# Weaving the first two chunks of three weight stages: w_out, w_up and the w_down quarters of a hybrid decoder layer

## The chip, the cores and the metric

One core of a Trainium2 chip runs the whole layer in one launch. The metric is the device time of that launch in microseconds (us); less is better. The kernel before takes 1529.46 us, the median of 3 runs (1527.65 to 1530.21).

## The reference, cut to what matters

One decoder layer over 256 tokens of width 2048, all in float32. Three branches (S5, RG-LRU, stick-breaking attention) are merged under gates; what matters here comes behind them:

```
merged = g_s5*(y_s5 @ w_br_s5) + g_lru*(y_lru @ w_br_lru) + g_attn*(y_attn @ w_br_attn)
h  = x + merged @ w_out                       # 2048 x 2048
hn = rms_norm(h, norm_mlp_g)
h  = h + (relu(hn @ w_up) ** 2) @ w_down      # 2048 x 8192, 8192 x 2048
out = rms_norm(h, final_norm_g)
```

## The kernel before, in words

**Units.** All weights come as one stream of units of 256 rows by 512 columns (512 KB). SP loads a unit into a raw tile (3 buffers, `load_next`, L110 to L120). `split_next` (L122) turns it into two float32r tiles: ScalarE (ACT) casts raw to hi (L135), VectorE (DVE) subtracts hi from raw and gets lo (L136); this subtraction is called the split below. TensorE then multiplies three times per operand pair: activation hi by weight hi (L213), hi by lo (L214), lo by hi (L215). One unit is 12 matmuls with 512 columns each. hi and lo have 3 buffers, so the cast of unit u waits until TensorE has done unit u-3, and runs in the time of unit u-2.

**Chunks.** `chunk_tok` (L204) computes 512 output columns for both blocks of 128 tokens into two PSUM banks. A chunk of w_out has 8 units (2048 rows). w_up has 16 chunks of 8 units, taken in four quarters; after each quarter of w_up, w_down takes the same quarter of the hidden channels: 4 chunks of 8 units, added to h_tok. `psm` has four banks of this kind.

**What stands between chunks.** The next stage contracts over the columns that a chunk just made, so they have to be transposed and split again before they can be an operand. That is side work, written as generators that are given to `later(gens, rate)` and advanced by `pump()` after each unit, `rate` steps per unit:

- `split_tok(c)` (L848): transposes a chunk of merged (16 DVE transposes of 32x256, four to a step), then splits it into mg_yhi and mg_ylo, the operand of w_out.
- `residual(c)` (L886): after a chunk of w_out is added to the residual (two h_tok additions on DVE, L899): 16 transposes into hT, then hhi (ACT, L883) and hlo (DVE, L884), the operand of w_up.
- `hidden` (L967): after the relu of a chunk of w_up (ACT, L986): 16 transposes into reluT, hd_hi (ACT square, L970), the same square on GpSimd (L971), and hd_lo (DVE, L974), the operand of w_down.
- `norm2` (L907): once the last residual is done, squares and sums hT, one small matmul for the sums over partitions (L914), an rsqrt. Its result is first used by the evacuation of w_down (L929).

The four chunks that feed a stage are read as kt 0 to 15, four kt to a chunk, two kt to a unit. So the last chunk's side work is due in unit 6 of the next stage's first chunk. `ms`, `hs` and `hs_` enforce that: at kt 12 they call `finish`, which issues what is left of the task. That is why the last task of each kind had rate 2:

```
    last = later([split_tok(3, ...)], 2.0)                          # L870
        rq = later([residual(c)], 2.0 if c == 3 else 1.0)           # L900
            hq = later([hidden(...)], 2.0 if c == FQ // CH - 1 else 1.0)   # L988
```

Each engine runs its instructions in order. What order the side work gets among the casts and splits is set where it is pumped, by `issue_after` on the unit's last cast, split and matmul.

Of the kernel before, what the change touches and what calls it, by code (L numbers as in the profile page):

```python
# [46 lines left out]
def hybrid_block(ctx: ExitStack, tc: tile.TileContext, io, out):  # L47
# [156 lines left out]
    def chunk_tok(name, c, k, xs, hold=0, done=None):  # L204
# [702 lines left out]
    def norm2():  # L907
        while rq[0]:
# [67 lines left out]
    for q in range(NQ):  # L976
        hd = {}
        for c in range(FQ // CH):
            banks = chunk_tok("w_up", q * (FQ // CH) + c, D, hs)
# [18 lines left out]
        for c in range(4):  # L998
            if q == NQ - 1 and c == 3:
                chunk_tok("w_down", c, FQ, hs_, HOLD, finish_tokens)  # L1000
                break
            banks = chunk_tok("w_down", c, FQ, hs_)
# [76 lines left out]
```

## Time and profile before

| | |
|---|---|
| median of 3 runs (lowest to highest) | 1529.46 us (1527.65 to 1530.21) |
| the profiled execution: its own time, its span | 1528.9 us, 1527.0 us |
| TensorE (PE) busy | 1491.6 us, 98% |
| VectorE (DVE) busy | 1170.1 us, 77% |
| ScalarE (ACT) busy | 780.2 us, 51% |
| GpSimd (POOL) busy | 113.2 us, 7% |
| DMA | 292.41 MB, mean 191 GB/s |
| granted TensorE clock, mean | 0.993 |

The span is the time from the first to the last instruction; the execution's own time is 1.9 us more. Busy times are sums over the whole span, and say nothing yet about who waits for whom: for that the waits and the timelines of single stages are read. A line "DVE L136 lo<-raw,hi" is the split of a unit.

### The profile page before, as it was taken

Reading aid. Unit: us, or ns where it says so; the run is one execution under the profiler, and the core shown is the slowest. Engines: PE = TensorE matmul, PEld = TensorE weight load, DVE = VectorE, ACT = ScalarE, POOL = GpSimd, SP = SyncE. Lnnn points to the kernel's source line nnn. Section 1 sums busy time; section 2 is a strip of 40 time slices with the busy share of each in tenths; the row PEclk is TensorE's granted clock in tenths of the full one; section 3 lists DMA queues with packets and bytes.
Section 4 is the critical chain, followed back from the end, with each engine's and each line's share of the span. In section 5 each row is a group of like instructions: output and inputs, shape, how many; then the busy total and the mean of one; then the engine's idle time right before and its main releaser. Section 6 shows DMA issues by size and latency. Waiting matters only on the chain.

```text
span 1527.0 us, 19937 instructions
## 1 busy us (share of the span) xinstructions
PE 1491.6 (98%) x7518; PEld 1261.0 (83%) x7518; DVE 1170.1 (77%) x1428; ACT 780.2 (51%) x918; POOL 113.2 (7%) x100
## 2 busy tenths in 40 slices
PE   9898999999998999999999999999999999999997
PEld 9896888989887877987788878888788887888786
DVE  5886998897988989688889885568754886558855
ACT  7478556565765564544346443344433443344443
POOL 6300000000000100001000000000100000000111
PEclk9999999999999999999999999999999999999999
DMA  9454766665565756665765656656566666666564
GB/s 290 143 173 143 227 209 193 194 184 167 172 184 168 209 184 204 187 203 182 250 200 184 184 181 210 191 187 193 193 193 193 192 194 186 195 187 198 176 203 152
DMA packets 88914, 292.41 MB, mean 191 GB/s; under 512 B 12786, under 2 KB 17010, under 8 KB 88562
## 3 DMA queue, kind: packets, MB, share of 16 engines
q1 hardware_dynamic: 88386, 287.93, 60.9%
q10 hardware_dynamic: 432, 3.21, 0.6%
q8 instruction: 59, 0.97, 0.3%
q14 instruction: 37, 0.30, 0.1%
HBM read 282.71 MB, written 2.10 MB: 187 GB/s over the span
## 4 chain that ended last, share of the span: by engine, by line
PE 83%; DVE 9%; ACT 3%; issue 3%; DMA 2%; SPq 0%; DVEq 0%; ACTq 0%
PE mt_w_up L215 7%; PE mt_w_up L214 7%; PE mt_w_up L213 7%; PE mt_w_down L214 7%; PE mt_w_down L215 7%; PE mt_w_down L213 7%; PE mt_w_in L214 5%; PE mt_w_in L215 5%; PE mt_w_in L213 5%; PE mm_w_in L198 4%; PE mm_w_in L199 4%; PE mm_w_in L197 4%; DVE lo L136 4%; ACT hi L135 2%; DVE reluT L683 1%
## 5 line engine op out<-in xcount | busy, mean ns | idle before, releaser
L136 DVE TENSOR_TENSOR lo<-raw,hi 128x1024 fp32r<-128x1024 f32 (+1 forms) x521 | 657.2, 1265 | 305.9 <-ACT hi L135 297.1
L135 ACT CAST hi<-raw 128x1024 fp32r<-128x1024 f32 (+1 forms) x521 | 545.5, 1049 | 643.3 <-PE mt_w_down L215 165.3
L214 PE MATMUL mt_w_down<-lo,hd_hi 128*128 128x512 f32 (+1 forms) x528 | 202.5, 384 | 5.6 <-DVE lo L136 5.6
L213 PE MATMUL mt_w_down<-hi,hd_hi 128*128 128x512 f32 (+1 forms) x528 | 202.1, 383 | 0.0
L215 PE MATMUL mt_w_down<-hi,hd_lo 128*128 128x512 f32 (+1 forms) x528 | 202.0, 383 | 0.0
L214 PE MATMUL mt_w_up<-lo,hhi 128*128 128x512 f32 x512 | 199.3, 389 | 0.0
L215 PE MATMUL mt_w_up<-hi,hlo 128*128 128x512 f32 x512 | 199.2, 389 | 0.0
L213 PE MATMUL mt_w_up<-hi,hhi 128*128 128x512 f32 x512 | 199.2, 389 | 0.0
L214 PE MATMUL mt_w_in<-lo,xhi 128*128 128x512 f32 x448 | 176.3, 394 | 4.2 <-DVE lo L136 4.1
L213 PE MATMUL mt_w_in<-hi,xhi 128*128 128x512 f32 x448 | 177.3, 397 | 2.9 <-ACT hi L135 2.9
L215 PE MATMUL mt_w_in<-hi,xlo 128*128 128x512 f32 x448 | 175.3, 391 | 0.0
L199 PE MATMUL mm_w_in<-xhi,lo 128*128 128x256 f32 x512 | 145.8, 286 | 3.1 <-DVE lo L136 3.0
L197 PE MATMUL mm_w_in<-xhi,hi 128*128 128x256 f32 x512 | 146.3, 286 | 1.7 <-DVE rs L298 0.9
L198 PE MATMUL mm_w_in<-xlo,hi 128*128 128x256 f32 x512 | 145.8, 285 | 0.0
L214 PEld LDWEIGHTS mt_w_down<-lo,hd_hi 128*128 128x128 f32 x528 | 99.2, 188 | 26.6 <-DVE lo L136 7.3
L213 PEld LDWEIGHTS mt_w_down<-hi,hd_hi 128*128 128x128 f32 x528 | 99.2, 188 | 19.5
L215 PEld LDWEIGHTS mt_w_down<-hi,hd_lo 128*128 128x128 f32 x528 | 99.2, 188 | 19.3
L683 DVE STREAM_TRANSPOSE reluT<-relu 32x256 f32<-32x256 f32 x256 | 111.5, 436 | 4.1
L214 PEld LDWEIGHTS mt_w_up<-lo,hhi 128*128 128x128 f32 x512 | 96.1, 188 | 20.1
L213 PEld LDWEIGHTS mt_w_up<-hi,hhi 128*128 128x128 f32 x512 | 96.1, 188 | 19.9
L215 PEld LDWEIGHTS mt_w_up<-hi,hlo 128*128 128x128 f32 x512 | 96.1, 188 | 19.9
L214 PEld LDWEIGHTS mt_w_in<-lo,xhi 128*128 128x128 f32 x448 | 84.6, 189 | 25.0 <-DVE lo L136 8.6
(278 smaller groups left out, 2039.5 us busy)
## 6 DMA issues: line engine op xcount, KB each, us to landing
raw<-in_w_in SPq DMA_DIRECT2D x175, 512.0 KB, 4.1
raw<-in_w_up SPq DMA_DIRECT2D x128, 512.0 KB, 4.0
raw<-in_w_down SPq DMA_DIRECT2D x128, 512.0 KB, 4.3
raw<-in_w_out SPq DMA_DIRECT2D x32, 512.0 KB, 4.3
raw<-in_w_br_lru SPq DMA_DIRECT2D x16, 512.0 KB, 4.2
raw<-in_w_br_attn SPq DMA_DIRECT2D x16, 512.0 KB, 4.1
raw<-in_w_br_s SPq DMA_DIRECT2D x16, 512.0 KB, 4.1
stk<-ux SPq DMA_DIRECT2D x96, 64.0 KB, 3.9
```

Of the source, the lines that this page charges most:

```text
L135: anchor["act"] = nc.scalar.copy(h[:, k, :], r[:, k, :]).ins
L136: anchor["dve"] = nc.vector.tensor_tensor(l_[:, k, :], r[:, k, :], h[:, k, :].bitcast(F32), ALU.subtract).ins
L197: nc.tensor.matmul(o, wh[:, kk, s], xh, start=first and ct % 2 == 0, stop=False, skip_group_check=True)
L198: nc.tensor.matmul(o, wh[:, kk, s], xl, start=False, stop=False, skip_group_check=True)
L199: mm = nc.tensor.matmul(o, wl[:, kk, s], xh, start=False, stop=last and ct % 2 == 1, skip_group_check=True)
L213: nc.tensor.matmul(banks[j], xh[:, s], wh[:, a:b], start=kt == 0, stop=False)
L214: nc.tensor.matmul(banks[j], xh[:, s], wl[:, a:b], start=False, stop=False)
L215: return nc.tensor.matmul(banks[j], xl[:, s], wh[:, a:b], start=False, stop=kt == ng * UK - 1)
L683: nc.vector.transpose(d_[32 * a:32 * a + 32, :, :, 32 * b:32 * b + 32], s_[32 * b:32 * b + 32, :, :, 32 * a:32 * a + 32])
```

## The change

In w_out, in the first quarter of w_up, and in each quarter of w_down, chunks 0 and 1 become a pair (`pair_tok`) that holds all four PSUM banks: units 0 to 5 of chunk 0, units 0 to 5 of chunk 1, then units 6 and 7 of chunk 0 and units 6 and 7 of chunk 1. The stream of loads is reordered in the same way (`add_pair`). kt 12 is now first read in unit 12 of sixteen. Chunk 0 is done after unit 14, chunk 1 after unit 16 (before: 8 and 16), and what follows a chunk (`out_done`, `up_done`, `down_done`) is the old code as a function. The three tasks that had rate 2 have rate 1. Quarters 1 to 3 of w_up keep their chunks one by one.

```diff
+    LATE = 2
+    def add_pair(name, c, k, g0=0):
+        ng = k // (P * UK)
+        for gs_ in (range(ng - LATE), range(ng - LATE, ng)):
+            stream.extend((name, c + i, g0 + g) for i in range(2) for g in gs_)
+    add_pair("w_out", 0, D)
+    for c in range(2, 4):
         add("w_out", c, D)
...
+        if q == 0:
+            add_pair("w_up", 0, D)
+        for c in range(0 if q else 2, FQ // CH):
             add("w_up", q * (FQ // CH) + c, D)
+        add_pair("w_down", 0, FQ, q * (FQ // (P * UK)))
...
+    def pair_tok(name, c, k, xs, done):
+        ng = k // (P * UK)
+        banks = [[psm.tile([P, CH], F32, tag="mm", ...) for t in range(2)] for i in range(2)]
+        for gs_ in (range(ng - LATE), range(ng - LATE, ng)):
+            for i in range(2):
+                for g in gs_:
+                    (nm, cc, _), wh, wl = next_unit()
...
+                    anchor["pe"] = mm.ins
+                    pump()
+                if gs_.stop == ng:
+                    done(c + i, banks[i])
...
-    last = later([split_tok(3, mlp.tile(...))], 2.0)
+    last = later([split_tok(3, mlp.tile(...))], 1.0)
...
-        rq = later([residual(c)], 2.0 if c == 3 else 1.0)
+        rq[0] = later([residual(c)], 1.0)
+    pair_tok("w_out", 0, D, ms, out_done)
+    for c in range(2, 4):
+        out_done(c, chunk_tok("w_out", c, D, ms))
...
-            hq = later([hidden(r, h_[:, k, :], l_[:, k, :], f"{q}_{c}")], 2.0 if c == FQ // CH - 1 else 1.0)
+            hq[0] = later([hidden(r, h_[:, k, :], l_[:, k, :], f"{q}_{c}")], 1.0)
+        if q == 0:
+            pair_tok("w_up", 0, D, hs, up_done)
...
+        pair_tok("w_down", 0, FQ, hs_, down_done)
```

The instructions are the same in kind and number, but for the grouping of transposes. Three places in DVE's order are shown, since DVE makes lo for TensorE and does the transposes. The number behind lo is the unit's place in the stream: w_out begins with 232, the first quarter of w_up with 264, the first quarter of w_down with 296. x8 is two steps of a task, or of two tasks, without anything between. Line numbers of the changed kernel are its own (L147 is the old L136, L716 the old L683, L917 the old L884, L933 the old L899, L1012 the old L974).

First place, DVE behind chunk 0 of w_out, the residual of chunk 0. Before:

```order
L136 TENSOR_TENSOR lo243_6816<-raw243_6795,hi243_6815 128x1024
L683 STREAM_TRANSPOSE hT_6622<-h_tok_6625 32x2x4x32 x4
L136 TENSOR_TENSOR lo244_6838<-raw244_6813,hi244_6837 128x1024
L683 STREAM_TRANSPOSE hT_6622<-h_tok_6625 32x2x4x32 x4
L136 TENSOR_TENSOR lo245_6860<-raw245_6835,hi245_6859 128x1024
L683 STREAM_TRANSPOSE hT_6622<-h_tok_6625 32x2x4x32 x4
L136 TENSOR_TENSOR lo246_6882<-raw246_6857,hi246_6881 128x1024
L683 STREAM_TRANSPOSE hT_6622<-h_tok_6625 32x2x4x32 x4
```

Now, units 17 to 22 of w_out, the residuals of chunks 0 and 1:

```order
L147 TENSOR_TENSOR lo249_6924<-raw249_6903,hi249_6923 128x1024
L716 STREAM_TRANSPOSE hT_6622<-h_tok_6625 32x2x4x32 x4
L933 TENSOR_TENSOR h_tok_6625<-mp_w_out_1_0_232_6629,xres_6619 128x512
L933 TENSOR_TENSOR h_tok_6625<-mp_w_out_1_1_232_6630,xres_6619 128x512
L147 TENSOR_TENSOR lo250_6950<-raw250_6921,hi250_6949 128x1024
L716 STREAM_TRANSPOSE hT_6622<-h_tok_6625 32x2x4x32 x4
L147 TENSOR_TENSOR lo251_6972<-raw251_6947,hi251_6971 128x1024
L716 STREAM_TRANSPOSE hT_6622<-h_tok_6625 32x2x4x32 x8
L147 TENSOR_TENSOR lo252_6998<-raw252_6969,hi252_6997 128x1024
L716 STREAM_TRANSPOSE hT_6622<-h_tok_6625 32x2x4x32 x8
L147 TENSOR_TENSOR lo253_7024<-raw253_6995,hi253_7023 128x1024
L917 SCALAR_TENSOR_TENSOR hlo_6624<-hT_6622,par_79,hhi_6623 128x256 x2
```

The two tasks have met: twice eight transposes stand between two splits, and after split 253 (unit 21) and split 254 an hlo pair of the first task and four transposes of the second stand together.

Second place, DVE in the first quarter of w_up, hidden tasks (relu0_0 is chunk 0, relu0_1 chunk 1). Before, chunk 1 alone:

```order
L136 TENSOR_TENSOR lo282_7682<-raw282_7656,hi282_7681 128x1024
L683 STREAM_TRANSPOSE reluT0_1_7697<-relu0_1_7674 32x2x4x32 x4
L136 TENSOR_TENSOR lo283_7705<-raw283_7679,hi283_7704 128x1024
L683 STREAM_TRANSPOSE reluT0_1_7697<-relu0_1_7674 32x2x4x32 x4
L136 TENSOR_TENSOR lo284_7727<-raw284_7702,hi284_7726 128x1024
```

Now, units 18 to 22 of w_up:

```order
L147 TENSOR_TENSOR lo282_7671<-raw282_7641,hi282_7670 128x1024
L716 STREAM_TRANSPOSE reluT0_0_7636<-relu0_0_7615 32x2x4x32 x4
L716 STREAM_TRANSPOSE reluT0_1_7690<-relu0_1_7663 32x2x4x32 x4
L147 TENSOR_TENSOR lo283_7698<-raw283_7668,hi283_7697 128x1024
L716 STREAM_TRANSPOSE reluT0_0_7636<-relu0_0_7615 32x2x4x32 x4
L716 STREAM_TRANSPOSE reluT0_1_7690<-relu0_1_7663 32x2x4x32 x4
L147 TENSOR_TENSOR lo284_7724<-raw284_7695,hi284_7723 128x1024
L716 STREAM_TRANSPOSE reluT0_1_7690<-relu0_1_7663 32x2x4x32 x4
L147 TENSOR_TENSOR lo285_7748<-raw285_7721,hi285_7747 128x1024
L716 STREAM_TRANSPOSE reluT0_1_7690<-relu0_1_7663 32x2x4x32 x4
L147 TENSOR_TENSOR lo286_7770<-raw286_7745,hi286_7769 128x1024
L1012 TENSOR_TENSOR hd_lo0_0_7614<-reluT0_0_7636,hd_hi0_0_7613 128x1024
```

Here too two tasks stand side by side: two groups of eight, where there were groups of four.

Third place, DVE at the start of the first quarter of w_down, the hidden task of the last w_up chunk. Before:

```order
L136 TENSOR_TENSOR lo298_8022<-raw298_7996,hi298_8021 128x1024
L683 STREAM_TRANSPOSE reluT0_3_8037<-relu0_3_8014 32x2x4x32 x8
L136 TENSOR_TENSOR lo299_8049<-raw299_8019,hi299_8048 128x1024
L683 STREAM_TRANSPOSE reluT0_3_8037<-relu0_3_8014 32x2x4x32 x8
L136 TENSOR_TENSOR lo300_8075<-raw300_8046,hi300_8074 128x1024
```

Now:

```order
L147 TENSOR_TENSOR lo298_8024<-raw298_7996,hi298_8023 128x1024
L716 STREAM_TRANSPOSE reluT0_3_8039<-relu0_3_8014 32x2x4x32 x4
L147 TENSOR_TENSOR lo299_8047<-raw299_8021,hi299_8046 128x1024
L716 STREAM_TRANSPOSE reluT0_3_8039<-relu0_3_8014 32x2x4x32 x4
L147 TENSOR_TENSOR lo300_8069<-raw300_8044,hi300_8068 128x1024
L716 STREAM_TRANSPOSE reluT0_3_8039<-relu0_3_8014 32x2x4x32 x4
L147 TENSOR_TENSOR lo301_8091<-raw301_8066,hi301_8090 128x1024
L716 STREAM_TRANSPOSE reluT0_3_8039<-relu0_3_8014 32x2x4x32 x4
L147 TENSOR_TENSOR lo302_8113<-raw302_8088,hi302_8112 128x1024
```

The sixteen transposes are spread over four units instead of two. It is the same in the other quarters.

## Rows read from the trace of the kernel before

In timelines the columns are: start in us from the span's start, duration in us (of a group of x instructions, of all of them), engine, line, operation, out<-in, shapes, count, and in brackets the idle time of the engine just before and what ended it.

**Rows 1.** The page's first part: span, and TensorE's busy time, share and instructions.
```profile
span 1527.0 us, 19937 instructions
PE 1491.6 (98%) x7518; PEld 1261.0 (83%) x7518; DVE 1170.1 (77%) x1428; ACT 780.2 (51%) x918; POOL 113.2 (7%) x100
```

**Rows 2.** The list of waits of TensorE from 722 us (start of w_out) to the end: who waited for whom, us in total, times, longest.
```profile
PE mt_w_down L214 <- DVE lo L136: 5.6, 4, 1.4
PE mt_w_out L214 <- DVE lo L136: 2.4, 3, 1.5
PE ps_n L914 <- DVE hT L313: 0.9, 1, 0.9
```

**Rows 3.** Timeline of TensorE: first matmul of w_down, the first matmul of its unit 4 and the two behind it; last, the same place in the fourth quarter.
```profile
901.77 0.39 PE L213 MATMUL mt_w_down<-hi,hd_hi 128*128 128x512 f32 x1
...
912.65 0.39 PE L213 MATMUL mt_w_down<-hi,hd_hi 128*128 128x512 f32 x1
914.44 0.50 PE L214 MATMUL mt_w_down<-lo,hd_hi 128*128 128x512 f32 x1 [1.40 <-DVE lo L136]
914.77 0.39 PE L215 MATMUL mt_w_down<-hi,hd_lo 128*128 128x512 f32 x1
...
1441.80 0.50 PE L214 MATMUL mt_w_down<-lo,hd_hi 128*128 128x512 f32 x1 [1.41 <-DVE lo L136]
```

**Rows 4.** Timeline of DVE at the same place, splits of units 2, 3, 4 and 5 of w_down and one of the two groups of transposes between them.
```profile
903.54 1.22 DVE L136 TENSOR_TENSOR lo<-raw,hi 128x1024 fp32r<-128x1024 f32 x1 [1.98 <-ACT hi L135]
...
908.28 1.22 DVE L136 TENSOR_TENSOR lo<-raw,hi 128x1024 fp32r<-128x1024 f32 x1
909.54 3.59 DVE L683 STREAM_TRANSPOSE reluT<-relu 32x256 f32<-32x256 f32 x8
913.16 2.36 DVE L136 TENSOR_TENSOR lo<-raw,hi 128x1024 fp32r<-128x1024 f32 x2
```

**Rows 5.** Timeline of DVE at the end of w_out: splits with an hlo pair between them, the additions behind the last chunk, and the split of unit 2 of w_up.
```profile
807.51 1.23 DVE L136 TENSOR_TENSOR lo<-raw,hi 128x1024 fp32r<-128x1024 f32 x1
808.65 0.87 DVE L884 SCALAR_TENSOR_TENSOR hlo<-hT,par,hhi 128x256 fp32r<-128x256 f32 x2
809.44 1.22 DVE L136 TENSOR_TENSOR lo<-raw,hi 128x1024 fp32r<-128x1024 f32 x1
...
812.85 1.28 DVE L899 TENSOR_TENSOR h_tok<-mt_w_out,xres 128x512 f32<-128x512 f32 x2
814.38 1.23 DVE L136 TENSOR_TENSOR lo<-raw,hi 128x1024 fp32r<-128x1024 f32 x1 [0.25 <-ACT hi L135]
```

**Rows 6.** Timeline of TensorE: first matmul of w_up, and the norm's small matmul with the one ahead of it.
```profile
813.09 0.39 PE L213 MATMUL mt_w_up<-hi,hhi 128*128 128x512 f32 x1
...
838.93 0.39 PE L213 MATMUL mt_w_up<-hi,hhi 128*128 128x512 f32 x1
840.24 0.58 PE L914 MATMUL ps_n<-ones,hT 128*128 128x1 f32 x4 [0.92 <-DVE hT L313]
```

**Rows 7.** Timeline of ACT in w_up: a cast with nothing in its way, the relu of chunk 0 and the cast behind it, the table load and the rsqrt of the norm, a hidden square.
```profile
816.01 1.05 ACT L135 CAST hi<-raw 128x1024 fp32r<-128x1024 f32 x1 [1.67 <-PE mt_w_up L215]
...
834.37 1.28 ACT L986 ACTIVATE relu<-mt_w_up 128x512 f32<-128x512 f32 x2 [0.28 <-PE mt_w_up L215]
835.55 1.06 ACT L135 CAST hi<-raw 128x1024 fp32r<-128x1024 f32 x1
...
839.37 1.28 ACT L296 ACT_TABLE_LOAD   x1
840.85 0.26 ACT L296 ACTIVATE rs<-ps_n,eps_t 128x2 f32<-128x2 f32 x1 [0.20 <-PE ps_n L914]
...
893.95 1.06 ACT L970 ACTIVATE hd_hi<-reluT 128x1024 fp32r<-128x1024 f32 x1 [1.81 <-DVE reluT L683]
```

**Rows 8.** Timeline of DVE in a w_up chunk with a hidden task at rate 1: two splits with four transposes between them, and a split a little later.
```profile
884.73 1.22 DVE L136 TENSOR_TENSOR lo<-raw,hi 128x1024 fp32r<-128x1024 f32 x1
885.98 1.78 DVE L683 STREAM_TRANSPOSE reluT<-relu 32x256 f32<-32x256 f32 x4
887.79 1.23 DVE L136 TENSOR_TENSOR lo<-raw,hi 128x1024 fp32r<-128x1024 f32 x1
...
895.99 2.15 DVE L136 TENSOR_TENSOR lo<-raw,hi 128x1024 fp32r<-128x1024 f32 x1 [0.81 <-ACT hi L135]
```

**Rows 9.** Timeline of GpSimd, two of its squares of reluT.
```profile
895.16 1.90 POOL L971 TENSOR_TENSOR reluT<-reluT 128x1024 f32<-128x1024 f32 x1 [19.62 <-ACT hd_hi L970]
914.36 2.91 POOL L971 TENSOR_TENSOR reluT<-reluT 128x1024 f32<-128x1024 f32 x1 [17.31 <-ACT hd_hi L970]
```

**Rows 10.** Timeline of TensorE in w_out: its first matmul, and the matmuls on lo of unit 5 and of unit 8.
```profile
722.72 0.39 PE L213 MATMUL mt_w_out<-hi,mg_yhi 128*128 128x512 f32 x1
...
738.84 0.50 PE L214 MATMUL mt_w_out<-lo,mg_yhi 128*128 128x512 f32 x1 [0.28 <-DVE lo L136]
...
747.86 0.50 PE L214 MATMUL mt_w_out<-lo,mg_yhi 128*128 128x512 f32 x1 [0.54 <-DVE lo L136]
```

**Rows 11.** Timeline of ACT in w_out: the casts of units 5 and 8.
```profile
736.48 1.05 ACT L135 CAST hi<-raw 128x1024 fp32r<-128x1024 f32 x1 [7.06 <-DMA raw<-in_w_out]
...
745.50 1.05 ACT L135 CAST hi<-raw 128x1024 fp32r<-128x1024 f32 x1 [4.81 <-DMA raw<-in_w_out]
```

**Rows 12.** DMA queues from 727 to 737 us: packets, MB, share of 16 engines. q10 is the queue on which ACT issues (here the residual input xres).
```profile
q10 hardware_dynamic: 144, 2.10, 58.2%
```

More of the change, by code (lines that the diff above doesn't have):

```diff
@@ L85, in hybrid_block @@
         add(*(("w_br_s5", int(a[1]), W) if a[0] == "b" else ("w_in", GATE0 + int(a[1]), D)))
-    for c in range(4):
+    LATE = 2
[5 more added lines that the diff above has]
+    for c in range(2, 4):
         add("w_out", c, D)
@@ L232, in chunk_tok @@
         return banks
+    def pair_tok(name, c, k, xs, done):
+        ng = k // (P * UK)
+        banks = [[psm.tile([P, CH], F32, tag="mm", name=f"mp_{name}_{c + i}_{t}_{st['use']}") for t in range(2)] for i in range(2)]
+        for gs_ in (range(ng - LATE), range(ng - LATE, ng)):
+            for i in range(2):
+                for g in gs_:
+                    (nm, cc, _), wh, wl = next_unit()
+                    assert (nm, cc) == (name, c + i)
+                    for kk in range(UK):
+                        kt = g * UK + kk
+                        xh, xl = xs(kt)
+                        for t in range(2):
+                            s = slice(t * P, (t + 1) * P)
+                            o = banks[i][t]
+                            nc.tensor.matmul(o, xh[:, s], wh[:, kk, :], start=kt == 0, stop=False)
+                            nc.tensor.matmul(o, xh[:, s], wl[:, kk, :], start=False, stop=False)
+                            mm = nc.tensor.matmul(o, xl[:, s], wh[:, kk, :], start=False, stop=kt == ng * UK - 1)
+                    anchor["pe"] = mm.ins
+                    pump()
+                if gs_.stop == ng:
+                    done(c + i, banks[i])
     par = const.tile([P, sum(PAR.values())], F32, name="par")
@@ L869, in hybrid_block @@
     nc.scalar.dma_start(x_tok, io["x_res"])
-    last = later([split_tok(3, mlp.tile([P, 4, L], F32, tag="reluT", name="mT3", bufs=2))], 2.0)
+    last = later([split_tok(3, mlp.tile([P, 4, L], F32, tag="reluT", name="mT3", bufs=2))], 1.0)
     hT = act.tile([P, KT, L], F32, tag="m16", name="hT")
@@ L894, in hybrid_block, with out_done @@
     rs2 = const.tile([P, 2], F32, name="rs2")
-    for c in range(4):
-        banks = chunk_tok("w_out", c, D, ms)
+    rq = [None]
+    def out_done(c, banks):
         s = slice(c * CH, (c + 1) * CH)
@@ L899, in hybrid_block @@
             nc.vector.tensor_tensor(h_tok[:, t, s], banks[t], x_tok[:, t, s], ALU.add)
-        rq = later([residual(c)], 2.0 if c == 3 else 1.0)
+        rq[0] = later([residual(c)], 1.0)
+    pair_tok("w_out", 0, D, ms, out_done)
+    for c in range(2, 4):
+        out_done(c, chunk_tok("w_out", c, D, ms))
     def hs(kt):
         if kt >= 12:
-            finish(rq)
+            finish(rq[0])
         return hhi[:, kt, :], hlo[:, kt, :]
     def norm2():
-        while rq[0]:
+        while rq[0][0]:
             yield
@@ L976, in hybrid_block, with up_done @@
     for q in range(NQ):
-        hd = {}
-        for c in range(FQ // CH):
-            banks = chunk_tok("w_up", q * (FQ // CH) + c, D, hs)
+        hd, hq = {}, [None]
+        def up_done(cu, banks):
+            c = cu % (FQ // CH)
             if c % 2 == 0:
@@ L997, in hybrid_block, with down_done @@
             finish(task)
[L998 to L1002, printed above, removed]
+        def down_done(c, banks):
             s = slice(c * CH, (c + 1) * CH)
@@ L1011, in hybrid_block @@
                     nc.gpsimd.tensor_tensor(ho[:, t, s], h_tok[:, t, s], gfb[:, s], ALU.mult)
+        pair_tok("w_down", 0, FQ, hs_, down_done)
+        for c in range(2, 4):
+            if q == NQ - 1 and c == 3:
+                chunk_tok("w_down", c, FQ, hs_, HOLD, finish_tokens)
+            else:
+                down_done(c, chunk_tok("w_down", c, FQ, hs_))
 def _lay_out(inp):
```

6 lines of the change are left out of this document (3 added, 3 removed).

## The prediction, as it was put on record

> **What bounds the kernel now.** I read the first part of the page first: TensorE is busy for 1491.6 of 1527.0 us [rows 1]. A change can win only idle time of TensorE, so the list of its waits comes next. From w_out to the end it names three: 5.6 us in w_down (4 times), 2.4 in w_out (3 times), 0.9 once at the norm [rows 2]. Each is followed into the timelines of TensorE, VectorE (DVE) and ScalarE (ACT).
>
> In w_down the reader is to see four units running at 2.72 us each (901.77 to 912.65), then a matmul on a lo tile 1.79 us after its predecessor, where 0.23 is the pitch [rows 3]. DVE was late: two groups of eight transposes stood between three splits [rows 4]. From that I take a rule of accounts for this kernel. The lo split of unit u starts, when nothing is in its way, 1.29 us after the start of unit u-2 (unit 0 of w_up starts at 813.09 [rows 6], the split for its unit 2 at 814.38 [rows 5]). The matmul that needs it starts 1.28 us after the split (913.16 [rows 4], 914.44 [rows 3]) and is due 0.23 into unit u. So a split may be late by 2 x 2.72 - 1.29 - 1.05 = **3.10 us** before TensorE waits.
>
> What DVE work between two splits costs against 2.72 us: four transposes make the pitch 3.06 (884.73 to 887.79 [rows 8]), so +0.35; eight make it 4.88 (908.28 to 913.16 [rows 4]), so +2.16; two hlo operations 1.93 (807.51 to 809.44 [rows 5]), so -0.79; hlo and four transposes 1.93 + 1.81 = 3.74, so +1.02. Test on the old kernel: split 2 of w_down is 903.54 - 901.77 - 1.29 = 0.48 late, split 3 2.50, split 4 4.66; less 3.10 is a wait of 1.56. The record has 1.79 - 0.23 = 1.56. After a wait the next matmul follows 0.34 behind instead of 0.23 [rows 3], 0.11 more.
>
> **1. w_down, removed.** The last hidden task now runs at rate 1: four groups of four transposes between splits 2 and 6, and its result is due in unit 12 instead of 6. Lateness 0.48 + 4 x 0.35 = 1.88, under 3.10. The same pattern stands in the old w_up [rows 8], where no wait of TensorE is listed [rows 2]. All four waits go: 4 x (1.56 + 0.11) = **-6.7 us**. The two evacuations that now stand two units apart (h_tok) meet no transposes, cost nothing.
>
> **2. Start of w_out, unchanged in the end.** Its groups of eight transposes go too. But what ends last there is a transfer: ACT waits 7.06 us until 736.48 for raw of unit 5 and until 745.50 for unit 8 [rows 11], while the residual input moves 2.10 MB on the other queue [rows 12]. The change moves neither that transfer nor gfb in ACT's order. Unit 5's matmul started at 738.84 as soon as its split allowed, unit 8's at 747.86, which is 3.15 late against 722.72 + 8 x 2.72 + 0.23 [rows 10]. Both dates come from the transfers and stay: **0**. If raw of unit 8 lands earlier, since raw of unit 7 is asked for 3 us sooner, up to -0.7.
>
> **3. End of the w_out pair, added.** Chunks 0 and 1 now end two units apart instead of eight, so their residual tasks, which never met before, run together. By the order, between splits 17 and 18 stand four transposes and the two h_tok additions of chunk 1 (1.28 [rows 5], 1.2 as pitch): 1.14 + 1.81 + 1.2 - 2.72 = 1.43 late. Then four (+0.35), eight (+2.16), eight (+2.16), hlo and four (+1.02), again (+1.02): lateness at split 23 is 8.14. Less 3.10, plus 0.11: **+5.1 us** of waits in units 20 to 23. After that the splits gain 0.79 each.
>
> **4. w_up pair, added.** The norm task now starts when the slower residual task has ended (unit 8) and runs in units 9 to 13; its sum is ready before TensorE reaches the norm's matmul, so its wait of 840.24 - 838.93 - 0.23 = **-1.08** [rows 6] goes. But the ACT table load (1.28) and the rsqrt (0.26) now stand before the relu of chunk 0. With the cast of unit 15 starting 0.20 into unit 13 (816.01 [rows 7], where unit 1 of w_up starts at 813.09 + 2.72 = 815.81) and 1.07 long, the relu pair starts 0.11 into unit 14 and takes 1.18 (834.37 to 835.55 [rows 7]); the cast of unit 16, and its split, are 1.10 late. Then the two hidden tasks overlap: +0.35 twice, +2.16 twice, +0.35 twice give 1.10 + 5.72 = 6.82 at split 22.
>
> Here GpSimd comes in. It squares reluT after the hd_hi activation. A split that started at 895.99 during such a square (895.16, 1.90 long) took 2.15 and ended at 898.14, 1.08 after the square's end; a square that started at 914.36 during a split took 2.91 [rows 8, 9]. Whoever starts second waits for the first. In the w_up pair the square of chunk 0 starts 1.21 after its hd_hi (893.95 [rows 7] to 895.16), which is 4.3 after the start of split 19 (1.25 + 1.81 + 1.21), and ends at 6.2; split 20 would start at 4.88 and end at 6.10, and ends at 7.3: +1.2. Sum: 6.82 + 1.2 - 3.10 + 0.11 = **+5.0 us**. The bounds for this collision are 0 (the square is the one that waits, as at 914.36) and 1.2; I take 1.2, since by the times the square starts first.
>
> The Trainium skill says in "SBUF — State Buffer", Who interferes with whom, that a DVE instruction with two SBUF inputs and a GpSimd instruction that reads SBUF exclude each other, and that the first to start keeps the shared port for its whole instruction. By that rule a split is held to the end of the square, and the sum has the 1.2; if the two shared the port in parts, a 1.90 us square over a 1.22 us split would cost less, and the sum would be nearer to +1.1 than to +2.3. The two stretched rows, 2.15 and 2.91, speak for the rule.
>
> **Sum.** -6.7 + 0 + 5.1 - 1.1 + 5.0 = **+2.3 us**. Matmuls (7518), casts, splits and transfers are the same in number; only their order moves. The profiled execution took 1528.9 us, so 1531.2; the median of the runs is 0.56 above it, 1529.46, and on it the forecast is **1531.8 us**. A measurement of this kernel can tell a difference from about 0.2% on, 3.06 us: below 1526.4 is faster, above 1532.5 slower. My forecast is no change that can be told, close to the slower side: the waits leave w_down and come back at the ends of two pairs.
>
> **Rivals.**
>
> A. *Slower, through a second square.* The square of chunk 1 is ready while DVE does hd_lo of chunk 0. If GpSimd takes its turn when that ends, split 23 is held for 1.90; split 22 and hd_lo take 2 x 1.13 (913.16, two in 2.36 [rows 4]) against 2.72, and the 0.11 counts too, so 0.57 of it is slack: +1.3, time 1533.1. By the Trainium skill's rule in the same section it happens if the square is the first to start. For it: the square asks 0.7 before split 23 is due. Against: at a pitch of 1.13 and a duration of 1.22 DVE leaves no gap between hd_lo and the split. It decides from 0.8 us up, as my sum stands that near to the bound. Chance 0.30, with other small stretches of this size in the two collisions.
>
> B. *Faster: the weaving spreads the work in w_out and w_up as well.* Were the backlogs of parts 3 and 4 under 3.10, the change would give -6.7 - 1.1 and up to -0.7: 1529.46 - 7.8 = 1521.7. For it: 16 units give a task more room than 8, and side tasks at rate 1 never made TensorE wait [rows 2, 8]. Against: the order shows groups of eight in both places, and one pair of such groups made every wait in w_down. Chance 0.08.
>
> C. *The w_down waits stay.* If four transposes per unit were late enough beside the evacuations, +6.7 would come on top: 1538.5. Against: [rows 8]. Chance 0.05.
>
> **Numbers.** The forecast with its own spread (0 to 1.2 for the square, -0.7 for raw of unit 8, some 1 us between medians) has 0.57, A 0.30, B 0.08, C 0.05. Part of the forecast's case lies beyond 1532.5 (0.07), part of A below it (0.06). So: faster 0.08, same 0.56, slower 0.36. The range reaches from 1528.5 (parts 2 and 4 at their low bounds, the median 1 us low) to 1534.8 (A, the median 1.7 us high) and leaves out B and C and a little of each side.
>
> **What would show it.** Right: no wait on lo in w_down; four waits of about 0.8, 2.2, 1.0 and 1.0 us near units 20 to 23 of w_out; a largest wait of some 3 us in w_up near unit 20, with a DVE split of more than 2 us beside a GpSimd square; none before the norm's matmul; unit 8 of w_out still about 3 us late. Wrong: waits in w_out's or w_up's pair under 2 us in sum (then B), or any in w_down (then C); a split stretched at unit 23 is A.

## The result and the profile after

The changed kernel takes **1531.61 us**, the median of 20 runs (1530.06 to 1534.78), against 1529.21 (20 runs, 1527.53 to 1530.61) for the old one: a ratio of 1.0016, 95% interval 1.001 to 1.0022, +2.4 us. Forecast were 1531.8 and no change that can be told. The slowdown is small, but with 20 runs a side the interval does not hold 1; it lies under the 0.2% that the forecast had set as its bound. The profiled execution took 1530.22 us with a span of 1528.5, which is 1.3 and 1.5 more than the old kernel's.

The first matmul of each stage, read from TensorE's timelines, gives this table. A stage has 32 units; at 2.72 each that is 87.05 us, its floor (87.6 for the last w_down, which is taken to its last matmul).

| from first matmul to first matmul, us | before | after | forecast of the difference | measured |
|---|---|---|---|---|
| w_out | 90.37 | 94.37 | +5.1 | +4.00 |
| w_up, first quarter | 88.68 | 93.32 | +3.9 | +4.64 |
| w_down, four quarters together | 355.60 | 348.75 | -6.7 | -6.85 |
| w_up, quarters 2 to 4, each | 87.04 | 87.04 | 0 | 0 |

The page's first part, against [rows 1]:

```profile
span 1528.5 us, 19943 instructions
PE 1492.3 (98%) x7518; PEld 1260.3 (82%) x7518; DVE 1175.2 (77%) x1428; ACT 780.0 (51%) x918; POOL 108.2 (7%) x100
```

TensorE does the same work, 7518 matmuls. The gain and the loss are mostly waits, so the list of TensorE's waits from 722 us on is next, against [rows 2]; columns: who waited for whom, us in total, times, longest.

```profile
PE mt_w_up L225 <- DVE lo L147: 4.0, 2, 3.0
PE mt_w_out L225 <- DVE lo L147: 2.5, 2, 1.9
PE mp_w_out L260 <- DVE lo L147: 0.8, 1, 0.8
PE mp_w_out L259 <- ACT hi L146: 0.5, 1, 0.5
```

No row names w_down, and none ps_n: these waits are gone, but for 0.2 us at ps_n. The waits on lo have moved to w_out and w_up. (mp_ is a matmul of a pair, mt_ one of a single chunk; the latter here stand in chunk 2, behind the pair.)

**w_down.** Timeline of DVE at the start of the first w_down, against [rows 4]: two splits with four transposes between them.

```profile
911.93 1.23 DVE L147 TENSOR_TENSOR lo<-raw,hi 128x1024 fp32r<-128x1024 f32 x1 [1.62 <-ACT hi L146]
913.07 1.77 DVE L716 STREAM_TRANSPOSE reluT<-relu 32x256 f32<-32x256 f32 x4
914.88 1.23 DVE L147 TENSOR_TENSOR lo<-raw,hi 128x1024 fp32r<-128x1024 f32 x1
```

The pitch is 2.95 in place of 4.88; DVE stays inside the 3.10 us that it may be late.

**End of the w_out pair.** Timeline of DVE, splits of units 19, 20 and 21 with the two groups of eight; the last row is the split of unit 23.

```profile
774.34 1.22 DVE L147 TENSOR_TENSOR lo<-raw,hi 128x1024 fp32r<-128x1024 f32 x1
775.60 3.58 DVE L716 STREAM_TRANSPOSE hT<-h_tok 32x256 f32<-32x256 f32 x8
779.21 1.23 DVE L147 TENSOR_TENSOR lo<-raw,hi 128x1024 fp32r<-128x1024 f32 x1
780.46 3.61 DVE L716 STREAM_TRANSPOSE hT<-h_tok 32x256 f32<-32x256 f32 x8
784.10 1.23 DVE L147 TENSOR_TENSOR lo<-raw,hi 128x1024 fp32r<-128x1024 f32 x1
...
791.80 1.23 DVE L147 TENSOR_TENSOR lo<-raw,hi 128x1024 fp32r<-128x1024 f32 x1
```

Timeline of TensorE at units 20 to 23 of the same stretch:

```profile
779.44 0.39 PE L224 MATMUL mt_w_out<-hi,mg_yhi 128*128 128x512 f32 x1
780.48 0.50 PE L225 MATMUL mt_w_out<-lo,mg_yhi 128*128 128x512 f32 x1 [0.66 <-DVE lo L147]
...
783.13 0.39 PE L224 MATMUL mt_w_out<-hi,mg_yhi 128*128 128x512 f32 x1
785.38 0.54 PE L225 MATMUL mt_w_out<-lo,mg_yhi 128*128 128x512 f32 x1 [1.86 <-DVE lo L147]
785.72 0.62 PE L226 MATMUL mt_w_out<-hi,mg_ylo 128*128 128x512 f32 x1
...
789.13 0.39 PE L225 MATMUL mt_w_out<-lo,mg_yhi 128*128 128x512 f32 x1
...
792.35 1.08 PE L224 MATMUL mt_w_out<-hi,mg_yhi 128*128 128x512 f32 x4
```

The reader is to see two waits, 0.81 and 2.02 us over the pitch (from start to start, less the 0.23 of matmuls that do not wait), where four were forecast (0.8, 2.2, 1.0, 1.0), and behind the second eight matmuls at a pitch of 0.43 instead of 0.23: from 785.72 to 789.13 they take 3.41 us, 1.60 more than eight at 0.227. Windows of 2 us (columns: window, its length, TensorE busy and matmuls begun, granted clock, DMA share, GB/s) tell why:

```profile
784.00:786.00 2.00, 0.62 (x2) 0.93 0.00 0
786.00:788.00 2.00, 2.00 (x6) 0.50 0.70 215
```

The granted clock fell to 0.50, the level of 1.2 GHz, after TensorE had stood for 1.86 us.

**The w_up pair.** Timeline of DVE, the splits of units 20, 23 and 24:

```profile
873.24 2.36 DVE L147 TENSOR_TENSOR lo<-raw,hi 128x1024 fp32r<-128x1024 f32 x1
...
881.67 1.22 DVE L1012 TENSOR_TENSOR hd_lo<-reluT,hd_hi 128x1024 fp32r<-128x1024 f32 x1
882.80 4.05 DVE L147 TENSOR_TENSOR lo<-raw,hi 128x1024 fp32r<-128x1024 f32 x2
```

GpSimd's two squares there, against [rows 9]:

```profile
872.62 1.89 POOL L1009 TENSOR_TENSOR reluT<-reluT 128x1024 f32<-128x1024 f32 x1 [146.09 <-issue]
881.66 2.97 POOL L1009 TENSOR_TENSOR reluT<-reluT 128x1024 f32<-128x1024 f32 x1 [7.15 <-ACT hd_hi L1008]
```

And TensorE, against [rows 6]: the norm's matmul, the wait of unit 20 and that of unit 23.

```profile
852.87 0.58 PE L952 MATMUL ps_n<-ones,hT 128*128 128x1 f32 x4
...
872.25 0.39 PE L224 MATMUL mt_w_up<-hi,hhi 128*128 128x512 f32 x1
875.65 0.50 PE L225 MATMUL mt_w_up<-lo,hhi 128*128 128x512 f32 x1 [3.01 <-DVE lo L147]
...
884.43 0.39 PE L224 MATMUL mt_w_up<-hi,hhi 128*128 128x512 f32 x1
885.77 0.50 PE L225 MATMUL mt_w_up<-lo,hhi 128*128 128x512 f32 x1 [0.95 <-DVE lo L147]
```

The norm's matmul comes 0.44 behind its predecessor (852.43), 0.2 over the pitch, where it waited 1.08. The split of unit 20 starts 0.62 after a square, takes 2.36 instead of 1.22, and TensorE waits 3.17 over the pitch at 872.25 to 875.65. The second square begins while DVE does hd_lo, lasts to 884.63, and the two splits behind take 4.05 instead of the 2.36 of two splits in [rows 4]: rival A's mechanism, 1.11 over the pitch at unit 23.

### The profile page after: what moved, and what is told of

The parts are those of the page before. It is cut to its first block, busy times and chain, and to the rows that moved or that the text cites. A ratio compares the mean times of both kernels' runs of the same rounds, so it can differ in the third digit from the quotient of the medians.

```text
span 1528.5 us, 19943 instructions
## 1 busy us (share of the span) xinstructions
PE 1492.3 (98%) x7518; PEld 1260.3 (82%) x7518; DVE 1175.2 (77%) x1428; ACT 780.0 (51%) x918; POOL 108.2 (7%) x100
## 4 chain that ended last, share of the span: by engine, by line
PE 82%; DVE 9%; ACT 3%; issue 3%; DMA 3%; SPq 0%; DVEq 0%; ACTq 0%
PE mt_w_up L225 6%; PE mt_w_up L226 6%; PE mt_w_up L224 6%; PE mt_w_in L225 5%; PE mt_w_in L226 5%; PE mt_w_in L224 5%; PE mp_w_down L261 4%; PE mp_w_down L260 4%; PE mp_w_down L259 4%; PE mt_w_down L225 4%; PE mt_w_down L224 4%; PE mt_w_down L226 4%; DVE lo L147 4%; PE mm_w_in L209 3%; PE mm_w_in L208 3%; PE mm_w_in L210 3%
## 5 line engine op out<-in xcount | busy, mean ns | idle before, releaser
L147 DVE TENSOR_TENSOR lo<-raw,hi 128x1024 fp32r<-128x1024 f32 (+1 forms) x521 | 662.7, 1274 | 310.0 <-ACT hi L146 304.0
L226 PE MATMUL mt_w_up<-hi,hlo 128*128 128x512 f32 x448 | 174.3, 389 | 0.0
L224 PE MATMUL mt_w_up<-hi,hhi 128*128 128x512 f32 x448 | 174.3, 389 | 0.0
L716 DVE STREAM_TRANSPOSE reluT<-relu 32x256 f32<-32x256 f32 x256 | 111.5, 436 | 4.2
L210 PEld LDWEIGHTS mm_w_in<-xhi,lo 128*128 128x128 f32 x512 | 98.6, 193 | 4.8 <-DVE lo L147 4.8
L225 PE MATMUL mt_w_down<-lo,hd_hi 128*128 128x512 f32 (+1 forms) x272 | 102.5, 377 | 0.0
L224 PE MATMUL mt_w_down<-hi,hd_hi 128*128 128x512 f32 (+1 forms) x272 | 102.4, 377 | 0.0
L226 PE MATMUL mt_w_down<-hi,hd_lo 128*128 128x512 f32 (+1 forms) x272 | 102.4, 376 | 0.0
L224 PEld LDWEIGHTS mt_w_in<-hi,xhi 128*128 128x128 f32 x448 | 84.3, 189 | 21.0 <-ACT hi L146 3.8
L208 PEld LDWEIGHTS mm_w_in<-xhi,hi 128*128 128x128 f32 x512 | 99.0, 193 | 3.1 <-ACT hi L146 1.5
L259 PE MATMUL mp_w_down<-hi,hd_hi 128*128 128x512 f32 x256 | 99.6, 389 | 0.0
L260 PE MATMUL mp_w_down<-lo,hd_hi 128*128 128x512 f32 x256 | 99.6, 389 | 0.0
```

Source lines behind the costliest of these rows:

```text
L147: anchor["dve"] = nc.vector.tensor_tensor(l_[:, k, :], r[:, k, :], h[:, k, :].bitcast(F32), ALU.subtract).ins
L208: nc.tensor.matmul(o, wh[:, kk, s], xh, start=first and ct % 2 == 0, stop=False, skip_group_check=True)
L210: mm = nc.tensor.matmul(o, wl[:, kk, s], xh, start=False, stop=last and ct % 2 == 1, skip_group_check=True)
L224: nc.tensor.matmul(banks[j], xh[:, s], wh[:, a:b], start=kt == 0, stop=False)
L225: nc.tensor.matmul(banks[j], xh[:, s], wl[:, a:b], start=False, stop=False)
L226: return nc.tensor.matmul(banks[j], xl[:, s], wh[:, a:b], start=False, stop=kt == ng * UK - 1)
```

## The experiments

Times are medians, with the ratio to the old kernel (in the same session) and its 95% interval. Stages are named by the time from first matmul to first matmul, as in the table above. The intervals are about 0.001 wide on either side, some 1.5 us, so smaller differences are read from the stages.

### One part at a time

Three kernels keep the pair in one kind of stage only. In the others the order of units and the rate of the task that feeds the stage are the old ones. For w_down only, against the full change:

```diff
-    pair_tok("w_out", 0, D, ms, out_done)
-    for c in range(2, 4):
+    for c in range(4):
         out_done(c, chunk_tok("w_out", c, D, ms))
...
-        if q == 0:
-            pair_tok("w_up", 0, D, hs, up_done)
-        for c in range(0 if q else 2, FQ // CH):
+        for c in range(FQ // CH):
...
-        rq[0] = later([residual(c)], 1.0)
+        rq[0] = later([residual(c)], 2.0 if c == 3 else 1.0)
```

and the same in the stream of loads and for split_tok(3). The other two are made alike (w_out only takes out the pairs of w_up and w_down, w_up only those of w_out and w_down).

w_down only:

> Only the four w_down stages have the pair; w_out and w_up go chunk by chunk as before, and split_tok(3) and residual(3) keep rate 2. My theory: the changed kernel's two halves are independent, and w_down alone wins what its stages won there, 4 times 1.70 us (92.81 to 91.1 a stage or 87.04 to 85.3 by the first matmuls), so about 1529.2 - 6.8 = 1522.4, with no wait on lo in w_down, and the waits of w_out and of the norm as in the old kernel. Rival 1: the pair itself costs something everywhere (four banks held at once, another order of loads), so that the gain is well under 6.8, above 1525. Rival 2: the waits come back elsewhere even so, near 1529.

Measured: 1521.07 us, 0.9942 (0.993 to 0.9954). Its list of waits from w_out on is

```profile
PE mt_w_out L222 <- DVE lo L144: 1.8, 2, 1.5
PE ps_n L948 <- DVE hT L343: 0.9, 1, 0.9
```

All w_down stages take 87.04, as in the full change: -6.8. The medians differ by 8.5. (By first matmuls a stage goes from 88.74 to 87.04, not from 87.04 to 85.3 as the expectation has it.) Of the rest, 0.9 us lies in w_out, 89.45 against 90.37, though its code is the old one: the cast of unit 8, which waits for a transfer, came at 744.12 here and at 745.50 before, and unit 8 lost nothing here. The pair costs nothing in w_down, where only one task runs.

w_out only:

> Only w_out has the pair; w_up and w_down are those of the old kernel, with rate 2 for the last hidden task and residual(3). My theory: the loss at the end of the w_out pair stays as in the changed kernel (w_out 90.37 to 94.37 us from its first matmul to that of w_up, +4.0), nothing is won behind it, so about 1529.2 + 4.0 = 1533.2; the list of waits has two on lo at units 20 and 21 of w_out, about 0.8 and 2.0 us, and the granted clock is 0.5 in the stretch behind the second. Rival: the loss depends on what comes behind it (the rate of residual(3), the norm), then w_out is as long as before and the time is near 1529.

Measured: 1533.69 us, 1.003 (1.0019 to 1.0042). w_out took 94.71 and w_up 89.36, 0.7 more than before; the rest is as before. The time fits. Against the expectation the clock stayed full, and there are four waits instead of two; what this means is seen in the experiment with the square on ACT.

w_up only:

> Only the first quarter of w_up has the pair, with residual(3) at rate 1; split_tok(3) and the last hidden task keep rate 2. My theory: that stage grows from 88.68 to about 93.3 us, +4.6, through the two hidden tasks that overlap and the two squares that hold splits 20 and 23, so about 1529.2 + 4.6 = 1533.8, and the three parts sum to the whole change (-6.8 + 4.0 + 4.6 = +1.8, and -0.25 ahead of w_out; 2.4 measured). Rival: the collision in w_up is a result of the lateness that w_out hands on (units 20 and 21 there), then this stage alone is less than 2 us longer and the time under 1531.5.

Measured: 1533.56 us, 1.0026 (1.0017 to 1.0036). w_up took 93.19 (+4.5), with its largest wait 3.17 over the pitch. So the loss in w_up is not handed on from w_out. In the stages that each one changed, the three differ from before by -6.8, +4.3 and +4.5, in sum +2.0, and the full change by +1.8: the parts add up. (The medians' differences, -8.5, +4.1 and +4.0, add up less well; the start of w_out, better in two of the three, is in them.)

### Two tasks one after the other

```diff
+    def queue(box, gen):
+        if box[0] is not None and box[0] in side:
+            box[0][0].append(gen)
+        else:
+            box[0] = later([gen], 1.0)
...
-        rq[0] = later([residual(c)], 1.0)
+        queue(rq, residual(c))
...
-            hq[0] = later([hidden(...)], 1.0)
+            queue(hq, hidden(...))
```

> The change in full, but the tasks of one kind stand in one queue: the residual (or hidden) task of chunk 1 begins when that of chunk 0 has ended, each one step per unit, and the point that makes an operand due waits for the tasks it needs. Only the overlap of two tasks is taken away; pairs, order of loads and banks stay. My theory (two groups of eight transposes in a row make DVE late): no group of eight is left, so the waits at units 20 to 23 of w_out and w_up go, with the half clock behind them; w_out falls from 94.4 to about 90 us and the first w_up from 93.3 to about 88, and the kernel comes to about 1531.6 - 4.4 - 4.8 = 1522.4, perhaps 1 us less. Rival: the pair's own form makes them (the late quarter of the operand, four banks held until the end, transposes beside evacuations), then the waits stay and the time is above 1529.

Measured: 1528.4 us, 0.999 (0.9981 to 0.9998). The waits at units 20 to 23 went, as forecast; the gain was 3 us, not 9. w_out took 91.82, w_up 90.78, the first w_down 88.71 (the others 87.04). Two reasons show. At the start of w_out the clock fell (0.50 from 741 to 743 us) after two waits of about 1 us: there the nine matmuls from 740.83 to 744.48 lost 1.6 us, where the full change has small waits of 0.7 us in sum. And in w_up the tasks follow each other without a free unit, as DVE's timeline shows:

```profile
879.04 1.22 DVE L147 TENSOR_TENSOR lo<-raw,hi 128x1024 fp32r<-128x1024 f32 x1
880.29 1.78 DVE L722 STREAM_TRANSPOSE reluT<-relu 32x256 f32<-32x256 f32 x4
882.11 1.23 DVE L147 TENSOR_TENSOR lo<-raw,hi 128x1024 fp32r<-128x1024 f32 x1
```

Each unit costs 3.07 against 2.72, and a lateness that is at its limit stays there: TensorE loses 0.1 to 0.3 us in most units from 869 us into the first w_down, and 0.9 us in units 26 to 28 of w_out. So the overlap is what makes the large waits, but my expectation left out that a lateness has to be paid back somewhere.

### The square on ACT

```diff
-        nc.gpsimd.tensor_tensor(rT, rT, rT, ALU.mult)
+        if name in ("0_0", "0_1"):
+            nc.scalar.activation(rT, rT, AF.Square)
+        else:
+            nc.gpsimd.tensor_tensor(rT, rT, rT, ALU.mult)
```

> The change, with one thing else: for chunks 0 and 1 of the first quarter of w_up the square of reluT, which GpSimd does, is done by ACT (activation Square in place). My theory (a split that meets a GpSimd square waits for its end): splits 20 and 23 of w_up are no longer stretched (2.36 and about 2.9 us, against 1.22), the wait at unit 20 falls from 3.17 to about 2.0 and that at unit 23 from 1.11 to near 0; the stage goes from 93.3 to about 91, the kernel from 1531.6 to about 1529.3. ACT has the time: it takes some 1.1 us more for each, twice. Rival: the splits are late through the transposes alone and the square only fills time in which DVE would have waited, then the stage stays within 0.5 us of 93.3 and the time near 1531.6. Second rival: the two squares make ACT's casts late, then waits on hi take the place of those on lo.

Measured: 1530.18 us, 1.0006 (0.9997 to 1.0014), with w_up at 90.84, **2.48 less** than in the full change (expected 2.4). Timelines of DVE (the split of unit 20) and of TensorE there:

```profile
876.65 1.23 DVE L147 TENSOR_TENSOR lo<-raw,hi 128x1024 fp32r<-128x1024 f32 x1
```

```profile
877.93 0.50 PE L225 MATMUL mt_w_up<-lo,hhi 128*128 128x512 f32 x1 [1.88 <-DVE lo L147]
```

The split is 1.23 long, the wait 2.04 over the pitch instead of 3.17, and unit 23 waits for nothing. So the square's hold on DVE is shown, and each of two costs 1.1 to 1.2 us. The Trainium skill's rule in "SBUF — State Buffer", SBUF: two separate sides, that the first to start keeps the shared port for its whole instruction, agrees with this trace: 2.36 falls to 1.23.

The same run answers what the half clock costs. It was not granted here, and w_out took 94.36, as in the full change (94.37). Timeline of TensorE at units 20 to 23 of w_out:

```profile
784.00 0.50 PE L225 MATMUL mt_w_out<-lo,mg_yhi 128*128 128x512 f32 x1 [0.66 <-DVE lo L147]
...
788.90 0.50 PE L225 MATMUL mt_w_out<-lo,mg_yhi 128*128 128x512 f32 x1 [1.84 <-DVE lo L147]
...
792.74 0.50 PE L225 MATMUL mt_w_out<-lo,mg_yhi 128*128 128x512 f32 x1 [0.56 <-DVE lo L147]
...
795.14 1.07 PE L224 MATMUL mt_w_out<-hi,mg_yhi 128*128 128x512 f32 x4
796.60 0.50 PE L225 MATMUL mt_w_out<-lo,mg_yhi 128*128 128x512 f32 x1 [0.39 <-DVE lo L147]
```

Here all four forecast waits stand: 0.81, 2.00, 0.73 and 0.55 over the pitch. In the full change the slow matmuls filled the time of the last two. DVE's dates were the same either way: its split of unit 23 came 69.3 us after the first matmul of w_out in both (791.80 - 722.47, and 795.32 - 725.98).

### The residual input later

```diff
-    nc.scalar.dma_start(x_tok, io["x_res"])
+    def x_load():
+        yield
+        yield
+        for c in range(4):
+            s = slice(c * CH, (c + 1) * CH)
+            nc.scalar.dma_start(x_tok[:, :, s], io["x_res"][:, :, s])
+            yield
+
+    later([x_load()], 0.5)
```

(and gfb is issued in quarter 2 of w_up.)

> The change, with one thing else: the residual input, 2.10 MB in one transfer ahead of w_out, is asked for in four slices of 0.52 MB through units 6 to 12 of w_out, and gfb 87 us and more later. My theory (the start of w_out is bound by transfers): the waits in units 5 to 8 (2.4 us with the small ones behind them, 0.9 on hi and 0.75 on lo the largest) go, w_out goes from 94.4 to about 92 us and the kernel to about 1529.2; the waits at units 20 and 21 stay, as they are DVE's. Rival: DVE or ACT bound these units anyway (the last groups of transposes of split_tok), then the waits stay within 0.5 us and the time with them. Second rival: the slices meet the loads of units 9 to 14 and the waits only move there.

Measured: 1528.93 us, 0.9999 (0.999 to 1.0008). w_out took 91.76, 2.6 less. The list of waits:

```profile
PE mt_w_out L225 <- DVE lo L147: 3.4, 4, 1.8
PE mt_w_up L225 <- DVE lo L147: 3.0, 1, 3.0
```

The waits at the start are gone, those of DVE's lateness all stay. So of the 7.32 us that w_out had over its floor after the change, 2.6 were the transfers' and 4.7 the pair's. The run moves two transfers, the residual input and gfb; how the 2.6 divide between them it does not show.

### Six units apart

```diff
+    PAIR = ((0, 0, 6), (1, 0, 2), (0, 6, 8), (1, 2, 8))
-        for gs_ in (range(ng - LATE), range(ng - LATE, ng)):
-            for i in range(2):
-                for g in gs_:
+        for i, a, b in PAIR:
+            for g in range(a, b):
...
-                if gs_.stop == ng:
+            if b == ng:
```

(in the stream of loads likewise.)

> The change with another order in the pairs: units 0 to 5 of chunk 0, units 0 and 1 of chunk 1, units 6 and 7 of chunk 0, then units 2 to 7 of chunk 1. The chunks end after units 10 and 16 of the pair, six units apart instead of two, and the last quarter of the operand is read from unit 8 on. Number of banks held, tasks, rates are the same. By the order of the instructions no two tasks' groups of four transposes then stand between two splits of w_out. My theory (it is the two tasks that overlap, not the pair): by the accounts of lateness the splits of w_out reach 2.4 us, under 3.10, so no wait at its end, w_out about 89.5 us (94.4); in w_up the norm task and the first hidden task still meet in units 12 to 14 (lateness 4.9, a wait of about 1.8, and up to 1.2 for a square), so about 90.5 us (93.3); w_down as in the change, no waits. In all about 1531.6 - 4.9 - 2.8 = 1524. Rival 1: the pair's own form costs (four banks, order of loads): w_out stays above 92 and the time above 1528. Rival 2: unit 8 is too early for the operand and w_down's waits come back, +1.5 us and more in each of its stages, about 1530.

Measured: 1524.64 us, 0.9971 (0.996 to 0.9983): w_out 89.79, w_up 91.21, each w_down 87.04. The list of waits has none on lo at the end of w_out:

```profile
PE ps_n L950 <- DVE hT L344: 1.0, 1, 1.0
PE mp_w_out L258 <- DVE lo L146: 0.8, 1, 0.8
PE mp_w_out L257 <- ACT hi L145: 0.7, 1, 0.7
PE mp_w_up L258 <- DVE lo L146: 0.6, 1, 0.6
```

Four banks are held and the tasks are the same; only the order of the units differs, and with it the distance between the ends of the two chunks and the unit that first reads the last quarter. It is the overlap, not the pair, that cost some 4.6 us in w_out (94.37 - 89.79). In w_up the waits are smaller and others than forecast (the norm's wait is back); 91.21 against 90.5.

### Two versions that beat both kernels

The mixed kernel has the order of the last experiment in w_out and w_down, single chunks in w_up, and the residual input later. Against the kernel of the last experiment:

```diff
-        if q == 0:
-            pair_tok("w_up", 0, D, hs, up_done)
-        for c in range(0 if q else 2, FQ // CH):
+        for c in range(FQ // CH):
...
-    nc.scalar.dma_start(x_tok, io["x_res"])
+    later([x_load()], 0.5)
...
-        rq[0] = later([residual(c)], 1.0)
+        rq[0] = later([residual(c)], 2.0 if c == 3 else 1.0)
```

(and gfb later, as there. Of the three tasks residual(3) alone has the old rate, 2.)

> The best that the accounts so far suggest: pairs in w_out and w_down only, in the order of six units apart (chunk 0 to unit 5, two units of chunk 1, the last two of chunk 0, the rest of chunk 1); w_up chunk by chunk as in the old kernel, with residual(3) at rate 2; and the residual input in four slices through units 6 to 12, gfb later. My theory: w_out near its floor of 87.05 us (32 units of 2.72, as the later w_up stages have it), w_up 88.7 as in the old kernel, w_down without waits, so about 1529.2 - 6.8 - 3.3 = 1519, 2 us under the kernel with pairs in w_down alone (1521.07). Rival: the gains at the start of w_out are the transfers' to give back (slices beside loads), or the earlier date, unit 8, makes the last split of the operand late; then it is at or above 1521.

Measured: 1520.67 us, 0.9943 (0.9929 to 0.9956), w_out 88.17 (expected near 87.05), w_up 88.81, w_down 87.04 each. One wait is left in the list:

```profile
PE ps_n L957 <- DVE hT L342: 1.0, 1, 1.0
```

By its time it cannot be told from the kernel with pairs in w_down only (0.9942); its w_out is 1.3 us shorter, its w_up 0.2 longer.

The last kernel is that of w_down only with the residual input later. Against that of w_down only (x_load is the one shown above, and gfb is later too):

```diff
-    nc.scalar.dma_start(x_tok, io["x_res"])
+    later([x_load()], 0.5)
```

> The kernel with pairs in w_down alone (w_out and w_up chunk by chunk, rates as in the old kernel), and the residual input in four slices through units 4 to 10 of w_out, gfb later. It asks what a pair in w_out is worth once the transfers are out of the way. My theory (in the old order too the start of w_out is bound by transfers, not by the side work at rate 2): w_out goes from 89.45 to about 88.2 us, as in the mixed kernel, which has a pair there, and the kernel from 1521.07 to about 1519.8, not to be told from the mixed one at 1520.67. Rival: the rate of 2 for split_tok binds as soon as the transfers don't (a group of eight transposes in unit 3, as in the old w_down), then waits on lo of 1.5 us and more stay, w_out is at or above 89.4 and the pair in w_out is what gave the mixed kernel its 88.17.

Measured: 1522.34 us, 0.9955 (0.9942 to 0.9969). w_out took 89.69: the rival held. (The four slices were asked for from 740.1 to 758.6 us, in units 5 to 12, not 4 to 10 as the expectation has it.) Timeline of DVE in unit 3 of w_out, a group of eight; for the split behind it, which starts at 735.28, TensorE waits 1.77 us:

```profile
731.67 3.58 DVE L713 STREAM_TRANSPOSE mT<-merged 32x256 f32<-32x256 f32 x8
```

At the start of w_out the transfers and the side work at rate 2 are two limits of nearly the same height. TensorE loses 2.6 us there with rate 1 alone (the full change), 2.4 with the later transfers alone (this kernel), and nothing with both (the residual input later, and the mixed kernel). Taking away either one alone wins nothing there or little.

## Why the prediction was right

The mechanisms of parts 1, 3 and 4 held; that of part 2 held only in half. That the time came out within 0.2 us is in part luck. Two errors nearly cancel (w_out too high by 1.1, w_up too low by 0.7), and the stages of the profiled runs differ by 1.8 us, not by the forecast 2.3, and their times by 1.3. The 2.4 between the medians rests on runs that have no trace (their clock is in the last section).

**Part 1, w_down, -6.7:** measured -6.85, and alone the same. All four waits went, no other came. The split of unit 6, the latest, was 1.78 late (924.10), forecast 1.88.

**Part 2, start of w_out, 0:** in the profiled runs the start had 3.32 us over its floor before (90.37 - 87.05) and 2.6 after. But the two kernels whose w_out is the old one had 2.4 there, so the change did not clearly move it. The reason that I gave, that transfers bind, is only half of it. I read units 5 and 8 and passed over unit 4, where TensorE had the longest of its three waits in w_out. Timelines of the old kernel there, DVE and TensorE:

```profile
730.86 3.58 DVE L683 STREAM_TRANSPOSE mT<-merged 32x256 f32<-32x256 f32 x8
734.47 1.23 DVE L136 TENSOR_TENSOR lo<-raw,hi 128x1024 fp32r<-128x1024 f32 x1
```

```profile
735.75 0.50 PE L214 MATMUL mt_w_out<-lo,mg_yhi 128*128 128x512 f32 x1 [1.54 <-DVE lo L136]
```

The split stood behind a group of eight, which the change takes away. In the changed kernel the transfer of unit 5 sets the date in its place. Timeline of ACT, the cast of unit 5:

```profile
735.64 1.05 ACT L146 CAST hi<-raw 128x1024 fp32r<-128x1024 f32 x1 [6.48 <-DMA raw<-in_w_out]
```

Nearly as much is lost, 2.6. So the 0 was right because the two limits lie close together, not because only one of them was there; in the last kernel, without the transfers, the groups of eight bind again.

**Part 3, end of the w_out pair, +5.1:** measured 4.75 (94.37 - 87.05 - 2.57). The lateness was right: the split of unit 23 is due 21 x 2.72 + 1.29 = 58.4 after the first matmul and came at 69.3; less the 2.57 lost at the start it was 8.35 late, forecast 8.14. What failed is the allowance of 3.10, which I took for all units. It holds where one hi matmul stands ahead of the first lo matmul. In unit 23 four stand ahead (792.35, x4), so the lo matmul is due 3 x 0.227 = 0.68 later. I read DVE's order for this and not TensorE's. With it, 5.15 - 0.68 + 0.33 (at full clock the 0.11 behind a wait comes four times, I counted it once) = 4.80.

**Part 4, w_up, -1.1 + 5.0:** measured +4.64 together. The norm's wait went, all but 0.2. The split of unit 16 was 857.45 - (816.84 + 14 x 2.72 + 1.29) = 1.24 late, forecast 1.10, but what ended last ahead of it was not quite what I had named. The table load and the rsqrt were done at 855.02, the date that I had for them; the relu still waited for TensorE, which was itself 0.77 late behind the norm's four matmuls in unit 13. Timeline of ACT, the relu:

```profile
855.21 1.28 ACT L1025 ACTIVATE relu<-mp_w_up 128x512 f32<-128x512 f32 x2 [0.19 <-PE mp_w_up L261]
```

The first square's hold was there (+1.1, forecast 1.2). The split of unit 22 was 880.52 - (816.84 + 20 x 2.72 + 1.29) = 7.99 late; the forecast's 6.82 and the square's 1.14 make 7.96. What this lateness costs was too high (4.3 in place of 5.0: the stage's 4.64, and the 0.84 that it gained at the norm, less 1.22 for the second square), since I counted it from TensorE's first matmul, and TensorE's own dates had moved back by the 0.77 of unit 13. And the second square, rival A's, added 1.2 that the forecast did not have. My ground against it, that DVE leaves no gap between hd_lo and the split, was wrong: the square began (881.66) as hd_lo did (881.67), and its 2.97 us are about hd_lo's 1.13 (its pitch) and its own 1.89: it was done between hd_lo and the split behind. The two starts lie too close to tell which was first; it was the square that waited.

**Rivals.** A: its mechanism happened; its time, 1533.1, did not, because w_out came out 1.1 lower (0.7 at its start, 0.4 at its end) and w_up, with both squares in it, 0.6 lower. B (no collisions) needed an order in which they don't meet; six units apart, it largely happens. C: excluded, no w_down wait came back.

## What to carry to other kernels

Weaving two chunks to give an operand more time also makes both chunks end together, and the work behind each end then meets: count, unit by unit, what the late engine has between two deadlines, and put the ends as far apart as one task is long (here six units in place of two). Use the pair only where the wait it removes is (w_down: -6.8 us), and read the order of the waiting engine as well as that of the late one. Where two limits have the same height, removing one shows nothing until the other goes too.

## What was not expected of the hardware

After the wait of 1.86 us in w_out the granted clock fell to 0.50 in the profiled run; after one of 3.01 us in w_up of the same run it did not, and in the kernel with the residual input later it was the other way round (0.50 from 876 to 878 us, in w_up); in the one with the pair in w_up only it fell in w_up as well (0.50 from 871 to 873). It cost nothing in these places, as w_up took 93.22 and 93.19 there and 93.32 in the full change: the slow matmuls took time in which TensorE would have waited at unit 23 (1.11 over the pitch in the full change, 0.18 and 0.24 in these two). At the start of w_out in the experiment with the tasks one after the other it was not covered in this way. Over whole runs the clock does go with the time: of the changed kernel's 20 runs the four with the lowest mean clock (0.989 to 0.991) are the four slowest, 1532.59 to 1534.78 us, and the one with the highest (0.996) is the fastest, 1530.06. Only one run of each kernel has a trace, so where those slower runs lost their time stays open.
